# A gated feed-forward stage on one core: four raw weight buffers, a stated order, token sums on VectorE, and the bias table moved to the first block

## The chip, the core and the metric

The kernel runs on one core of a Trainium2 chip. Its engines work side by side, each through an instruction queue of its own and in order: TensorE (PE in the profile), VectorE (DVE), ScalarE (ACT), GpSimd (POOL), and SyncE (SP), which here only starts transfers. The metric is the device time of one execution, in microseconds. A median over runs is given for the kernel before; the profile shows one execution.

## The reference

One step of a decoder trunk with two layers over 576 tokens (512 of a prompt, 64 of samples) and 1024 features. The part that the change touches is the gated feed-forward block, which runs four times, and the relative bias of the attention.

```python
def rms_norm(x, g):
    xf = x.astype(jnp.float32)
    y = xf * lax.rsqrt(jnp.mean(xf * xf, axis=-1, keepdims=True) + RMS_EPS)
    return (y * g.astype(jnp.float32)).astype(x.dtype)

def swiglu(x, wi, wo):
    gate, up = jnp.split(x @ wi, 2, axis=-1)
    return (jax.nn.silu(gate) * up) @ wo
...
        bias = rel_bias[t5_buckets(offs)][:, g * ATTN_HEADS:(g + 1) * ATTN_HEADS].astype(f32)
...
        h = h + 0.5 * swiglu(rms_norm(h, w['norm_w'][i, 0]), w['ffn1_wi'][i], w['ffn1_wo'][i])
...
        h = h + mix
        h = h + 0.5 * swiglu(rms_norm(h, w['norm_w'][i, 2]), w['ffn2_wi'][i], w['ffn2_wo'][i])
        h = h + jax.nn.sigmoid(rms_norm(h, w['norm_w'][i, 3]) @ w['pe_gate'][i]) * (p[i] @ w['pe_proj'][i])
```

The inner width is 2816, that is 22 tiles of 128. Layer 0 mixes by a recurrence (RWKV), layer 1 by windowed attention with three groups of windows; `bias` is the table of relative biases of one group.

## The kernel before

**Tiling.** Activations lie with features on the 128 partitions and the 576 tokens along the row, in two halves of 288 (`HF`). Every float32 operand is split in two parts, H (a rounded copy, made by ScalarE's cast) and L (the rest, a subtraction), and a product is three matmuls: H with H, H with L, L with H. So each raw weight tile of 128 x 512 costs a transfer (SyncE), a cast (ScalarE) and a subtraction (GpSimd, or VectorE for some).

**Stages.** `run` (L1653) goes: block A (first feed-forward of layer 0), RWKV, block B (second of layer 0), the gated extra input and the shared keys and values, block C (first of layer 1), attention, block D (second of layer 1), final norm. All four blocks are `ffn` (L352).

**A block.** The 22 pairs of a gate tile and an up tile come in order. Pairs 0 to 4 are plain (`pair`, L359): gate and up products into the four banks `ps_e`, VectorE evicts the gate sums times rs (L364), ScalarE takes silu (L150), GpSimd multiplies by rs again (L367), VectorE multiplies into the up sums (L370). Pairs 0 and 4 go through all four banks at once, so they need all four free. During pairs 0 to 4, `forms` (L283) prepares token sums for what follows: two scalings (L294) and four subtractions for each of four feature pairs, VectorE and GpSimd in turn (L296 to L299), and their splits (L157).

Pairs 5 to 21 (`pair7`, L379) do the 2 x 2 block product in seven products (L389) instead of eight. `seven` (L314) loads four raw blocks (L324: two from the three buffers `wr`, which the plain weights share, two from the three buffers `sr`), makes sums of weights s1, s2 and s4 on VectorE (L336) and s3 on GpSimd (L345), and splits the seven forms (casts L330 on ScalarE, subtractions L331). A pair's evictions are, in order: copies L395, L398, L401 on ScalarE, L403 on VectorE, L406 and L408 on VectorE, silu L150, L411 on GpSimd and L412 on VectorE. The banks of these products are the same `ps_e`, and two of another pool `ps_d`.

After pairs 7, 14 and 21 an output part (`wo_part`, L415) multiplies the finished tiles by their output weights (L168, L171, L172, L198, and L421 adds to the residual). The pair loop runs one pair ahead of it: pair 7 is done before the first output part, pair 8 comes behind it.

**The bias table.** `bias_table` (L1278) is called three times in block B, after pairs 2, 5 and 8. Each call makes 1160 columns in four chunks of 290: a one-hot chunk is loaded from ScalarE's queue (L1285, one buffer), one matmul into `ps_q` (L1287), a copy to `tb` (L1288), then a transfer of the table (L1289), and two reversed halves by copy (L1293) and transfer (L1294).

**Order.** A scheduler with a priority heap lays out each engine's queue at build time, from the order in which the code is written and from when operands and buffers come free in its plan. What an engine does next on the chip is that fixed order: an instruction that waits holds all behind it on its engine. Besides, the code can state an order between two instructions by hand.

## Time and profile before

| | us |
|---|---|
| median of three runs | 2956.97 (2955.53 to 2964.45) |
| the profiled execution | 2955.22 |
| its span in the trace | 2953.4 |
| busy: PE, POOL, DVE, ACT | 2757.3, 1568.7, 1528.6, 1299.3 |
| block A, pairs to last output part | about 30 to 444 |
| block B | about 1130 to 1563 |
| block C | about 1647 to 2067 |
| block D | about 2471 to 2888 |

How to read it: the table's last four lines are places in the span. TensorE's busy time also counts the slow stretches, in which its granted clock (PEclk in a window's row) is 0.50. A row of waits tells who released the waiting instruction last; the engine named may itself have waited for another.

### The profile page before, as it was taken

What the parts mean: (1) busy time and instruction counts of PE and PEld (TensorE: products, weight loads), DVE (VectorE), ACT (ScalarE), POOL (GpSimd) and SP (SyncE); (2) the same over time, 40 slices, a digit from 0 to 9 for tenths busy, and PEclk for the clock granted to TensorE, in tenths of its full rate; (3) what the DMA queues carried; (4) which work ended last, traced back from release to release, by engine and by line L of the source; (5) the groups of instructions that cost most, each with busy time, mean ns of one, the idle gap of its engine ahead of it and who ended that gap; (6) DMA issues with size and microseconds to landing.
All of it is one profiled execution on the core that took longest, in us unless ns stands there. A gap on an engine that the chain in (4) does not pass through costs nothing.

```text
span 2953.4 us, 56222 instructions
## 1 busy us (share of the span) xinstructions
PE 2757.3 (93%) x21958; PEld 2565.7 (87%) x21958; DVE 1528.6 (52%) x3192; ACT 1299.3 (44%) x2532; POOL 1568.7 (53%) x1300
## 2 busy tenths in 40 slices
PE   7899997998999999999999989999899999899997
PEld 7899996986767778889999989999888889899997
DVE  6432428557677756433436543243477775533435
ACT  4443435444333324434445444354455655434444
POOL 6655647544243337656654566564544326756653
PEclk9999998998999999999999999999999999999999
DMA  3222234222112112222233222223433443232223
GB/s 117 75 89 84 87 95 145 65 68 54 53 45 77 42 49 77 76 82 85 91 94 101 88 76 93 80 86 108 125 81 98 127 151 109 70 90 86 93 79 101
DMA packets 177580, 257.83 MB, mean 87 GB/s; under 512 B 47037, under 2 KB 71537, under 8 KB 177313
## 3 DMA queue, kind: packets, MB, share of 16 engines
q1 hardware_dynamic: 148736, 223.56, 25.4%
q10 hardware_dynamic: 28576, 30.66, 3.8%
q8 instruction: 173, 2.83, 0.4%
q14 instruction: 95, 0.77, 0.1%
HBM read 234.31 MB, written 19.85 MB: 86 GB/s over the span
## 4 chain that ended last, share of the span: by engine, by line
PE 70%; DVE 11%; issue 6%; POOL 6%; DMA 4%; ACT 3%; SPq 0%; DVEq 0%; ACTq 0%; POOLq 0%
PE ps_e L198 25%; PE ps_e L389 20%; PE ps_d L516 9%; PE ps_d L389 3%; PE ps_i L516 2%; PE ps_q L516 2%; PE ps_s L516 2%; PE ps_w L516 2%; POOL wl L172 1%; POOL wl L331 1%; PE ps_x L516 1%; PE ps_o L516 1%; PE ps_d L198 1%; DVE S L1303 1%; PE ps_pt L525 1%
## 5 line engine op out<-in xcount | busy, mean ns | idle before, releaser
L172 POOL TENSOR_TENSOR wl<-wr,wh 128x512 fp32r<-128x512 f32 (+2 forms) x477 | 598.9, 1265 | 694.4 <-ACT wh L171 653.9
L198 PE MATMUL ps_e<-hv,wh 128*128 128x288 f32 x2944 | 588.5, 295 | 2.5 <-ACT wh L171 1.3
L171 ACT CAST wh<-wr 128x512 fp32r<-128x512 f32 (+2 forms) x477 | 277.1, 586 | 573.6 <-PE ps_e L198 298.0
L198 PEld LDWEIGHTS ps_e<-hv,wh 128*128 128x128 f32 x2944 | 472.9, 188 | 3.8 <-POOL hv L157 2.2
L198 PE MATMUL ps_e<-hv,wl 128*128 128x288 f32 x1472 | 434.2, 295 | 1.2 <-POOL wl L172 1.2
L198 PE MATMUL ps_e<-x,wh 128*128 128x288 f32 x1792 | 371.0, 302 | 25.3 <-DVE u L370 12.8
L516 PE MATMUL ps_d<-x,wh 128*128 128x288 f32 x1664 | 369.1, 309 | 7.5 <-DVE q L1371 3.8
L198 PEld LDWEIGHTS ps_e<-x,wh 128*128 128x128 f32 x1792 | 296.3, 193 | 30.3 <-issue 15.2
L516 PEld LDWEIGHTS ps_d<-x,wh 128*128 128x128 f32 x1664 | 274.7, 192 | 28.1 <-issue 9.5
L198 PEld LDWEIGHTS ps_e<-hv,wl 128*128 128x128 f32 x1472 | 276.8, 188 | 1.5 <-POOL wl L172 1.4
L198 PE MATMUL ps_e<-x,wl 128*128 128x288 f32 x896 | 268.4, 300 | 1.6 <-POOL wl L172 1.6
L389 PE MATMUL ps_e<-x,wh 128*128 128x288 f32 x1088 | 230.2, 305 | 31.5 <-DVE ev L406 18.4
L421 DVE SCALAR_TENSOR_TENSOR h<-ps_e,h 128x288 f32<-128x288 f32 x192 | 87.6, 456 | 325.9 <-PE ps_e L198 325.7
L516 PE MATMUL ps_d<-x,wl 128*128 128x288 f32 x832 | 250.6, 302 | 0.3 <-POOL wl L172 0.3
L389 PEld LDWEIGHTS ps_e<-x,wh 128*128 128x128 f32 x1088 | 180.8, 195 | 37.0 <-DVE ev L406 21.4
L331 POOL TENSOR_TENSOR wl<-wr,wh 128x512 fp32r<-128x512 f32 x136 | 177.8, 1310 | 11.1 <-ACT wh L330 9.9
L330 ACT CAST sh<-ps_q 128x512 fp32r<-128x512 f32 x136 | 79.9, 588 | 222.3 <-DVE ps_q L336 184.7
L331 POOL TENSOR_TENSOR wl<-ss,wh 128x512 fp32r<-128x512 f32 x68 | 88.6, 1302 | 166.4 <-ACT wh L330 156.4
L198 PEld LDWEIGHTS ps_e<-x,wl 128*128 128x128 f32 x896 | 172.4, 193 | 2.1 <-POOL wl L172 2.0
L389 PE MATMUL ps_e<-TH,wh 128*128 128x288 f32 x544 | 162.2, 298 | 12.9 <-ACT ev L395 11.2
L389 PE MATMUL ps_e<-x,wl 128*128 128x288 f32 x544 | 164.8, 303 | 0.0
L331 DVE TENSOR_TENSOR wl<-ps_q,wh 128x512 fp32r<-128x512 f32 x68 | 47.0, 691 | 222.2 <-ACT wh L330 222.2
(394 smaller groups left out, 6700.8 us busy)
## 6 DMA issues: line engine op xcount, KB each, us to landing
wr<-in_f1wi SPq DMA_DIRECT2D x108, 256.0 KB
wr<-in_f2wi SPq DMA_DIRECT2D x108, 256.0 KB
sr<-in_f1wi SPq DMA_DIRECT2D x68, 256.0 KB
sr<-in_f2wi SPq DMA_DIRECT2D x68, 256.0 KB
wr<-in_f1wo SPq DMA_DIRECT2D x64, 256.0 KB
wr<-in_f2wo SPq DMA_DIRECT2D x64, 256.0 KB
wr<-in_wrkv SPq DMA_DIRECT2D x48, 256.0 KB
wr<-in_wq SPq DMA_DIRECT2D x48, 256.0 KB
```

Of the source, the lines that this page charges most:

```text
L171: nc.scalar.copy(H, raw)
L172: nc.gpsimd.tensor_tensor(L, raw, H.bitcast(F32), op=ALU.subtract)
L198: nc.tensor.matmul(ps[0:nw], a, b[:, sl], start=k + m == 0, stop=3 * k + m == n - 1)
L330: nc.scalar.copy(H, a)
L331: eng.tensor_tensor(L, a, H.bitcast(F32), op=ALU.subtract)
L389: nc.tensor.matmul(ps, a, b, start=first and k + m == 0, stop=k == DT // 2 - 1 and m == 2, skip_group_check=True)
L421: nc.vector.scalar_tensor_tensor(h[:, sl], ps, 0.5, h[:, sl], op0=ALU.mult, op1=ALU.add)
L516: self.nc.tensor.matmul(out, lhsT, rhs, **kw)
L525: self.nc.tensor.transpose(out, in_, ident)
L1303: nc.vector.tensor_tensor_reduce(dst, ps, bias, -1.0, 3.0e38 if mx is None else mx, op0=ALU.add, op1=ALU.min, accum_out=m)
```

## The change

It does four things. The raw buffers `wr` and `sr` go from three to four. A stated order (`after`) puts each pair's s1 behind the last up eviction of the pair two before on VectorE, its first cast behind that pair's silu on ScalarE, its s3 behind that pair's last split on GpSimd, and half of the first splits of the quarters behind pair 4's last up eviction. The token sums are VectorE's alone (their splits GpSimd's), and so is the product t*rs of the plain pairs. The bias table is made in block A, after pairs 9, 12 and 16, in three chunks of 387 into `ps_d`, with the one-hot rows of a group loaded by one transfer ahead, and one reversed copy.

```diff
+B_MID = (9, 12, 16)
...
+    def after(self, ins, other):
+        self.tc.add_manual_dep(ins, other.name, mybir.DependencyInfo(mybir.DependencyClass.NoSync, mybir.DependencyReason.DATA), reason="order")
...
-            raw = self.wp.tile([128, c * nw], F32, name="wr", tag="wr", bufs=N_W - 1)
+            raw = self.wp.tile([128, c * nw], F32, name="wr", tag="wr", bufs=N_W)
...
             nc.vector.tensor_tensor(c[:, h0], a[:, h1], a[:, h0], op=sub)
-            nc.gpsimd.tensor_tensor(c[:, h1], b[:, h1], a[:, h1], op=sub)
+            nc.vector.tensor_tensor(c[:, h1], b[:, h1], a[:, h1], op=sub)
             nc.vector.tensor_tensor(d, b[:, h1], c[:, h0], op=sub)
-            nc.gpsimd.tensor_tensor(a[:, h1], b[:, h0], d, op=sub)
+            nc.vector.tensor_tensor(a[:, h1], b[:, h0], d, op=sub)
...
-            self.split(d, H[:, 2], L[:, 2])
+            self.split(d, H[:, 2], L[:, 2], nc.gpsimd)
...
-                    self.split(xn[k][z], H, L, (nc.vector, nc.gpsimd)[k % 2])
+                    if k % 2:
+                        self.split(xn[k][z], H, L, nc.gpsimd)
+                    else:
+                        nc.scalar.copy(H, xn[k][z])
+                        i = nc.vector.tensor_tensor(L, xn[k][z], H.bitcast(F32), op=sub).ins
+                        if z:
+                            self.after(i, self.last_u)
...
-    def seven(self, w0, w1):
+    def seven(self, w0, w1, prev):
...
-                r = self.ph.tile([128, n], F32, name="sr", tag="sr", bufs=3)
+                r = self.ph.tile([128, n], F32, name="sr", tag="sr", bufs=N_W)
             else:
-                r = self.wp.tile([128, n], F32, name="wr", tag="wr", bufs=N_W - 1)
+                r = self.wp.tile([128, n], F32, name="wr", tag="wr", bufs=N_W)
...
-            nc.scalar.copy(H, a)
+            c = nc.scalar.copy(H, a).ins
+            if not i and prev:
+                self.after(c, prev[1])
...
+            if op == ALU.add and prev:
+                self.after(i, prev[0])
...
+        if prev and prev[2]:
+            self.after(i, prev[2])
...
                 if half:
-                    self.act(t1, t1, AF.Silu)
-                    nc.gpsimd.tensor_tensor(t1, t1, rs, op=ALU.mult)
+                    hist[j] = [self.act(t1, t1, AF.Silu)]
+                    (nc.vector if fast else nc.gpsimd).tensor_tensor(t1, t1, rs, op=ALU.mult)
...
+            hist[j] = self.last_u, hist[j][0], None
...
-            W = self.seven(wi[j], wi[FT + j])
+            W = self.seven(wi[j], wi[FT + j], hist[j - 2])
...
+            hist[j] = i, silu, self.last_l
...
-                if mid and j in (2, 5, 8):
-                    mid(j // 3)
+                if mid and j in B_MID:
+                    mid(B_MID.index(j))
...
+    def bias_rows(self, g):
+        self.oh = self.sm("oh", [33, TBW])
+        self.nc.scalar.dma_start(self.oh, self.I["onehot"][g])
...
-        for c in range(0, TBW, 290):
-            e = min(c + 290, TBW)
-            oh = self.sm("oh", [33, 290])
-            nc.scalar.dma_start(oh[:, 0:e - c], self.I["onehot"][g][:, c:e])
-            ps = self.bank("q", e - c)
-            nc.tensor.matmul(ps[0:16], self.rb[:, g * 16:(g + 1) * 16], oh[:, 0:e - c], start=True, stop=True)
+        for c in range(0, TBW, 387):
+            e = min(c + 387, TBW)
+            ps = self.pg.tile([128, e - c], F32, name="ps_d", tag="d")
+            nc.tensor.matmul(ps[0:16], self.rb[:, g * 16:(g + 1) * 16], oh[:, c:e], start=True, stop=True)
             nc.vector.tensor_copy(tb[:, c:e], ps[0:16])
+        if g < 2:
+            self.bias_rows(g + 1)
         nc.scalar.dma_start(self.tab[g * 16:(g + 1) * 16], tb)
-        n = SKW // 2
-        for c in (0, n):
-            tr = self.sm("tr", [16, n])
-            nc.vector.tensor_copy(tr, tb[:, TBW - 1 - c - n:TBW - 1 - c][:, ::-1])
-            nc.scalar.dma_start(self.rev[g * 16:(g + 1) * 16, c:c + n], tr)
+        tr = self.sm("tr", [16, SKW])
+        nc.vector.tensor_copy(tr, tb[:, TBW - 1 - SKW:TBW - 1][:, ::-1])
+        nc.scalar.dma_start(self.rev[g * 16:(g + 1) * 16], tr)
...
-            self.ffn(I["f1wi"][0], I["f1wo"][0], lambda: self.feed(spill=True), pre, fast="n00")
+            self.bias_load()
+            self.ffn(I["f1wi"][0], I["f1wo"][0], lambda: self.feed(spill=True), pre, self.bias_table, fast="n00")
...
-                self.bias_load()
-                self.ffn(I["f2wi"][0], I["f2wo"][0], lambda: self.feed("n03"), self.pre, self.bias_table, fast="n02")
+                self.ffn(I["f2wi"][0], I["f2wo"][0], lambda: self.feed("n03"), self.pre, fast="n02")
```

Line numbers move: the changed kernel has L300 to L305 for the sums (L294 to L299 before), L336 for the raw loads (L324), L345 for the splits (L331), L350 for s1, s2 and s4 (L336), L361 for s3 (L345), L382 for the gate eviction (L364), L385 for t*rs (L367), L388 for the up eviction (L370), L408 for the seven products (L389), L414, L417, L420, L422, L425, L427 and L431 for the evictions of a seven-product pair (L395, L398, L401, L403, L406, L408, L412), and L441 for the output parts (L421).

**VectorE around pair 3 in block A.** The numbers behind a name tell one tile from another: hv_607 and hv_608 (hv_614 and hv_615 in the changed kernel) are the scaled features of the last token sums, t1_623 (t1_630) the gate tile of pair 3, u_624 (u_631) its up tile. Before:

```order
L294 SCALAR_TENSOR_TENSOR hv_607<-h1_104,vecs_66,rs_165 128x576
L298 TENSOR_TENSOR u_596<-hv_592,t1_595 128x288
L294 SCALAR_TENSOR_TENSOR hv_608<-h3_146,vecs_66,rs_165 128x576
L296 TENSOR_TENSOR t1_611<-hv_607 128x288
L157 TENSOR_TENSOR TL2_602<-u_596,TH2_601 128x288
L298 TENSOR_TENSOR u_612<-hv_608,t1_611 128x288
L364 TENSOR_TENSOR t1_623<-ps_e_649,rs_165 128x288
L364 TENSOR_TENSOR t1_623<-ps_e_675,rs_165 128x288
L157 TENSOR_TENSOR TL3_618<-u_612,TH3_617 128x288
L370 TENSOR_TENSOR u_624<-ps_e_703,t1_623 128x288
```

The same place now:

```order
L300 SCALAR_TENSOR_TENSOR hv_614<-h1_104,vecs_66,rs_165 128x576
L305 TENSOR_TENSOR hv_598<-hv_599,u_603 128x288
L300 SCALAR_TENSOR_TENSOR hv_615<-h3_146,vecs_66,rs_165 128x576
L302 TENSOR_TENSOR t1_618<-hv_614 128x288
L303 TENSOR_TENSOR t1_618<-hv_615,hv_614 128x288
L304 TENSOR_TENSOR u_619<-hv_615,t1_618 128x288
L382 TENSOR_TENSOR t1_630<-ps_e_656,rs_165 128x288
L305 TENSOR_TENSOR hv_614<-hv_615,u_619 128x288
L382 TENSOR_TENSOR t1_630<-ps_e_682,rs_165 128x288
L385 TENSOR_TENSOR t1_630<-t1_630,rs_165 128x576
L388 TENSOR_TENSOR u_631<-ps_e_710,t1_630 128x288
```

The two splits (TL) have left VectorE; the subtractions L303 and L305 and the product L385 have come, one L305 between the two gate evictions.

**SyncE's queue behind the first output part of block A.** The names wr and sr are raw weights; 1833, 1835, 1837 and 1839 are pair 8's four blocks, 1983 to 1989 pair 9's, and from 2133 pair 10's (in the changed kernel 1840 to 1846, 1990 to 1996, and from 2156). Before:

```order
L168 DMA wr_1775<-in_f1wo 128x512
L168 DMA wr_1781<-in_f1wo 128x384
L324 DMA wr_1833<-in_f1wi 128x512
L324 DMA wr_1837<-in_f1wi 128x512
L324 DMA wr_1983<-in_f1wi 128x512
L324 DMA sr_1989<-in_f1wi 128x512
L324 DMA wr_1987<-in_f1wi 128x512
L324 DMA sr_2135<-in_f1wi 128x512
L324 DMA sr_2139<-in_f1wi 128x512
```

The same place now:

```order
L174 DMA wr_1782<-in_f1wo 128x512
L174 DMA wr_1788<-in_f1wo 128x384
L336 DMA wr_1840<-in_f1wi 128x512
L336 DMA wr_1844<-in_f1wi 128x512
L336 DMA sr_2158<-in_f1wi 128x512
L336 DMA wr_1990<-in_f1wi 128x512
L336 DMA wr_1994<-in_f1wi 128x512
L336 DMA wr_2156<-in_f1wi 128x512
L336 DMA sr_2162<-in_f1wi 128x512
```

Both `sr` blocks of pair 9 are loaded before the output weights now, a block of pair 10 stands ahead of pair 9's two `wr` blocks, and these two follow each other.

**VectorE in pair 8.** 2145 (2168 in the changed kernel) is s1 of pair 10; 1949, 1877 and 1878 (1956, 1884 and 1885) are what pair 8's evictions write. Before:

```order
L403 TENSOR_TENSOR t1_1877<-ps_d_1881,ev_1894 128x288
L336 TENSOR_TENSOR ps_q_2145<-sr_2135,wr_2137 128x512
L331 TENSOR_TENSOR sl_2020<-ps_q_2017,sh_2019 128x512
L406 TENSOR_TENSOR ev_1949<-ps_e_1879,ev_1908 128x288
L408 TENSOR_TENSOR t1_1877<-ps_e_1880,ev_1922 128x288
L331 TENSOR_TENSOR sl_2148<-ps_q_2145,sh_2147 128x512
L336 TENSOR_TENSOR ps_q_2151<-ps_q_2145,wr_2133 128x512
L412 TENSOR_TENSOR u_1878<-ps_e_1879,t1_1877 128x288
```

The same place now:

```order
L422 TENSOR_TENSOR t1_1884<-ps_d_1888,ev_1901 128x288
L345 TENSOR_TENSOR sl_2027<-ps_q_2024,sh_2026 128x512
L425 TENSOR_TENSOR ev_1956<-ps_e_1886,ev_1915 128x288
L427 TENSOR_TENSOR t1_1884<-ps_e_1887,ev_1929 128x288
L431 TENSOR_TENSOR u_1885<-ps_e_1886,t1_1884 128x288
L350 TENSOR_TENSOR ps_q_2168<-sr_2158,wr_2160 128x512
L345 TENSOR_TENSOR sl_2171<-ps_q_2168,sh_2170 128x512
```

The first sums of pair 10's weights stood among pair 8's evictions and stand behind the last of them now.

## Rows read from the trace of the kernel before

**Rows 1.** The page's first part: busy time, share of the span, instructions of each engine.

```profile
PE 2757.3 (93%) x21958; PEld 2565.7 (87%) x21958; DVE 1528.6 (52%) x3192; ACT 1299.3 (44%) x2532; POOL 1568.7 (53%) x1300
```

**Rows 2.** Waits of PE, whole run: waiting line, its releaser, total us, times, longest.

```profile
PE ps_e L389 <- DVE ev L406: 18.4, 11, 3.3
...
PE ps_e L389 <- DVE t L364: 13.1, 3, 4.9
PE ps_e L198 <- DVE u L370: 12.8, 4, 4.2
PE ps_e L389 <- ACT ev L395: 11.2, 8, 2.1
...
PE ps_q L1287 <- DMA oh<-in_onehot: 7.7, 5, 1.9
...
PE ps_e L198 <- ACT TH L156: 2.8, 3, 1.1
...
PE ps_q L1287 <- DVE tb L1288: 2.1, 1, 2.1
```

**Rows 3.** Windows: us; busy of PE, PEld, DVE, ACT, POOL; PEclk, DMA share, GB/s.

```profile
76.03:82.86 6.83, 5.40 (x22) 5.43 (x23) 2.70 (x3) 1.34 (x2) 5.06 (x4) 0.50 0.17 46
...
192.09:195.50 3.41, 3.41 (x16) 3.41 (x15) 1.53 (x3) 1.50 (x3) 1.20 (x2) 0.50 0.25 77
...
sum 68.26, PE 57.45 PEld 53.12 DVE 37.08 ACT 26.48 POOL 37.02; mean PE 4.42 PEld 4.09 DVE 2.85 ACT 2.04 POOL 2.85
```

**Rows 4.** Timeline, end of pair 3: start, us, engine, line, operation, [idle before <-releaser].

```profile
61.36 1.53 DVE L157 TENSOR_TENSOR hv<-u,hv 128x576 fp32r<-128x576 f32 x1 [0.74 <-ACT hv L156]
...
69.18 1.55 DVE L157 TENSOR_TENSOR TL<-u,TH 128x288 fp32r<-128x288 f32 x1
...
71.63 0.81 DVE L364 TENSOR_TENSOR t<-ps_e,rs 128x288 f32<-128x288 f32 x2
...
72.85 0.68 ACT L150 ACTIVATE t<-t 128x576 f32<-128x576 f32 x1
...
75.43 1.39 POOL L367 TENSOR_TENSOR t<-t,rs 128x576 f32<-128x576 f32 x1
...
76.86 0.82 DVE L370 TENSOR_TENSOR u<-ps_e,t 128x288 f32<-128x288 f32 x2 [2.51 <-POOL t L367]
...
77.46 0.82 PE L198 MATMUL ps_e<-x,wh 128*128 128x288 f32 x2 [4.21 <-DVE u L370]
```

**Rows 5.** Timeline of DVE, pair 4.

```profile
93.50 0.90 DVE L336 TENSOR_TENSOR ps_q<-sr,wr 128x512 f32<-128x512 f32 x1 [1.69 <-DMA wr<-in_f1wi]
...
95.66 0.81 DVE L364 TENSOR_TENSOR t<-ps_e,rs 128x288 f32<-128x288 f32 x2
```

**Rows 6.** Timelines of four engines, first pairs after an output part.

```profile
172.07 0.70 DVE L336 TENSOR_TENSOR ps_q<-sr,wr 128x512 f32<-128x512 f32 x1 [5.01 <-DMA wr<-in_f1wi]
...
175.24 1.30 POOL L331 TENSOR_TENSOR wl<-wr,wh 128x512 fp32r<-128x512 f32 x1
...
176.57 0.33 SPq L324 DMA_DIRECT2D wr<-in_f1wi  x1
...
179.72 0.70 DVE L336 TENSOR_TENSOR ps_q<-sr,wr 128x512 f32<-128x512 f32 x1 [2.98 <-DMA wr<-in_f1wi]
...
182.95 0.40 PE L389 MATMUL ps_e<-TH,wh 128*128 128x288 f32 x1 [2.08 <-ACT ev L395]
...
189.94 0.70 DVE L336 TENSOR_TENSOR ps_q<-sr,wr 128x512 f32<-128x512 f32 x1 [2.89 <-DMA wr<-in_f1wi]
```

**Rows 7.** Single lines: count, ns min/median/max, first and last start, forms.

```profile
L298 DVE TENSOR_TENSOR u<-hv,t x16: 446/696/1146, 40.2 to 2517.0; 128x288 f32<-128x288 f32 x16
...
L367 POOL TENSOR_TENSOR t<-t,rs x20: 1387/1430/1515, 33.5 to 2546.5; 128x576 f32<-128x576 f32 x20
```

**Rows 8.** Timeline of ACT's queue, one group of the bias table.

```profile
1214.34 6.22 ACTq L1285 DMA_DIRECT2D oh<-in_onehot  x3
```

**Rows 9.** Timeline of DVE, pair 7, no stall.

```profile
131.70 0.46 DVE L408 TENSOR_TENSOR t<-ps_e,ev 128x288 f32<-128x288 f32 x1 [1.16 <-PE ps_e L389]
```

More of the change, by code (lines that the diff above doesn't have):

```diff
@@ L152, in act @@
         self.agrp.append(i)
+        return i
+    def after(self, ins, other):
+        self.tc.add_manual_dep(ins, other.name, mybir.DependencyInfo(mybir.DependencyClass.NoSync, mybir.DependencyReason.DATA), reason="order")
     def split(self, src, H, L, eng=None):
@@ L156, in split @@
         nc.scalar.copy(H, src)
-        (eng or nc.vector).tensor_tensor(L, src, H.bitcast(F32), op=ALU.subtract)
+        self.last_l = (eng or nc.vector).tensor_tensor(L, src, H.bitcast(F32), op=ALU.subtract).ins
         return H, L
@@ L335, in diff @@
             t = self.bank("q")
-            nc.vector.tensor_tensor(t, a, b, op=op)
+            i = nc.vector.tensor_tensor(t, a, b, op=op).ins
+            if op == ALU.add and prev:
+                self.after(i, prev[0])
             return t
@@ L344, in seven @@
         s3 = self.ph.tile([128, n], F32, name="ss", tag="ss", bufs=1)
-        nc.gpsimd.tensor_tensor(s3, raw["11"], raw["21"], op=ALU.subtract)
+        i = nc.gpsimd.tensor_tensor(s3, raw["11"], raw["21"], op=ALU.subtract).ins
+        if prev and prev[2]:
+            self.after(i, prev[2])
         form(4, s3, nc.gpsimd)
@@ L355, in ffn @@
         xs, rs = self.xl[0], self.rs
-        hv = {}
+        hv, hist = {}, {}
         self.n_hv, self.n_t1 = N_HF, 4
@@ L365, in ev_g @@
                 if half:
-                    self.act(t1, t1, AF.Silu)
-                    nc.gpsimd.tensor_tensor(t1, t1, rs, op=ALU.mult)
+                    hist[j] = [self.act(t1, t1, AF.Silu)]
+                    (nc.vector if fast else nc.gpsimd).tensor_tensor(t1, t1, rs, op=ALU.mult)
             def ev_u(half, ps, sl):
-                nc.vector.tensor_tensor(u[:, sl], ps, t1[:, sl], op=ALU.mult)
+                self.last_u = nc.vector.tensor_tensor(u[:, sl], ps, t1[:, sl], op=ALU.mult).ins
             last = fast and j == F_STD - 1
@@ L408, in pair7 @@
             nc.vector.tensor_tensor(t1[:, h1], C, u2, op=ALU.add)
-            self.act(t1, t1, AF.Silu)
+            silu = self.act(t1, t1, AF.Silu)
             prod(A, 6, 3, False)
             nc.gpsimd.tensor_tensor(u[:, h1], c22, t1[:, h1], op=ALU.mult)
-            nc.vector.tensor_tensor(u[:, h0], A, t1[:, h0], op=ALU.mult)
+            i = nc.vector.tensor_tensor(u[:, h0], A, t1[:, h0], op=ALU.mult).ins
             hv[j] = self.split(u, self.s("hv", self.n_hv, F32R), self.s("hv", self.n_hv, F32R), nc.gpsimd)
+            hist[j] = i, silu, self.last_l
         def wo_part(js, last):
@@ L720, in weights @@
                 if n not in wl:
-                    raw = self.wp.tile([128, 512], F32, name="wr", tag="wr", bufs=N_W - 1)
+                    raw = self.wp.tile([128, 512], F32, name="wr", tag="wr", bufs=N_W)
                     H = self.wp.tile([128, 512], F32R, name="wh", tag="wh")
@@ L1276, in bias_load @@
         self.rev = self.dr.tile([48, SKW], F32, name="rev")
+        self.bias_rows(0)
+    def bias_rows(self, g):
+        self.oh = self.sm("oh", [33, TBW])
+        self.nc.scalar.dma_start(self.oh, self.I["onehot"][g])
     def bias_table(self, g):
         nc = self.nc
+        oh = self.oh
         tb = self.sm("tb", [16, TBW])
-        for c in range(0, TBW, 290):
-            e = min(c + 290, TBW)
-            oh = self.sm("oh", [33, 290])
-            nc.scalar.dma_start(oh[:, 0:e - c], self.I["onehot"][g][:, c:e])
-            ps = self.bank("q", e - c)
-            nc.tensor.matmul(ps[0:16], self.rb[:, g * 16:(g + 1) * 16], oh[:, 0:e - c], start=True, stop=True)
+        for c in range(0, TBW, 387):
+            e = min(c + 387, TBW)
+            ps = self.pg.tile([128, e - c], F32, name="ps_d", tag="d")
+            nc.tensor.matmul(ps[0:16], self.rb[:, g * 16:(g + 1) * 16], oh[:, c:e], start=True, stop=True)
             nc.vector.tensor_copy(tb[:, c:e], ps[0:16])
+        if g < 2:
+            self.bias_rows(g + 1)
         nc.scalar.dma_start(self.tab[g * 16:(g + 1) * 16], tb)
-        n = SKW // 2
-        for c in (0, n):
-            tr = self.sm("tr", [16, n])
-            nc.vector.tensor_copy(tr, tb[:, TBW - 1 - c - n:TBW - 1 - c][:, ::-1])
-            nc.scalar.dma_start(self.rev[g * 16:(g + 1) * 16, c:c + n], tr)
+        tr = self.sm("tr", [16, SKW])
+        nc.vector.tensor_copy(tr, tb[:, TBW - 1 - SKW:TBW - 1][:, ::-1])
+        nc.scalar.dma_start(self.rev[g * 16:(g + 1) * 16], tr)
     def softmax(self, S, parts, n, adds):
```

## The prediction

> **What bounds the kernel now.** I read the page's busy line first: TensorE is busy 93% of the span and every other engine about half of it [rows 1]. So the time is TensorE's work plus TensorE's holes, and the change takes away none of that work. Next come TensorE's waits over the whole run [rows 2]. Five of the lines belong to the gated feed-forward blocks (four of them, called A to D in order): the last sums of a product that VectorE has not evicted (L406, 18.4 us), gate sums not evicted (L364, 13.1), up sums not evicted (L370, 12.8), copies by ScalarE not done (L395, 11.2), and in block B alone a one-hot chunk not landed (L1287, 7.7) or a table copy late (2.1). With L156 (2.8) that is 68.4 us, all of it in stretches which the change touches. Third is the granted clock. In 13 stretches of the four blocks it is 0.50, the 1.2 GHz level, and they begin in or right after such holes [rows 3]: two of the holes below end at 77.46 and near 192, and stretches begin at 76.03 and 192.09. TensorE was busy for 57.45 us in them; at 2.4 GHz that work takes half, so the holes cost 28.7 us a second time.
>
> Then the timeline around three holes, for who is late and why.
>
> **Start of the seven-product pairs** (blocks A, C, D, and hidden in B). TensorE has finished pair 3, and pair 4 wants four banks at once. VectorE evicts the gate sums only at 71.63, since the token sums fill it; silu runs at 72.85; the product t*rs stands on GpSimd behind two splits and runs at 75.43; the up sums leave at 76.86 and TensorE goes on at 77.46 [rows 4]. A pair later VectorE stands in front of s1 of pair 6, which waits for its raw weights until 93.50, and the gate eviction behind it comes at 95.66 [rows 5].
>
> **First pairs after an output part** (twice in each block). The raw buffer that s1 of pair 9 needs is free when GpSimd has split pair 8's (175.24 + 1.30 = 176.54), its load is issued at 176.57, and s1 runs at 179.72. ScalarE's cast of s1 is queued ahead of its copy L395 of pair 8, so TensorE waits 2.08 us. At 189.94 s1 of pair 10 is late in the same way, and VectorE's L406 stands behind it [rows 6].
>
> **The change, part by part.**
>
> *Token sums and t*rs.* Between the up sums of pair 2 and the last gate eviction of pair 3, VectorE has four scalings, four subtractions and one split; now four scalings and seven subtractions, with the splits on GpSimd. A subtraction on VectorE is 0.70 us (median of L298 [rows 7]) and the split was 1.55: 3 x 0.70 - 1.55 = +0.6 us [rows 4]. So the gate sums leave no earlier than before, rather 0.6 us later, silu at about 73.4. What is won is behind it: t*rs runs directly on VectorE. Its price there is not in the trace; its nearest rows are L157's split of the same size on VectorE at 61.36 (1.53 us, from beside a busy GpSimd [rows 4]) and twice the shortest half-size subtraction, 2 x 0.45 = 0.9 [rows 7]; I take 1.5, the row of the same size. The up sums then leave at 73.4 + 0.7 + 1.5 = 75.6 instead of 76.86, and the hole of 1.1 + 4.2 = 5.3 becomes about 4.0. GpSimd is now free of 32 subtractions and 20 products of 1.43 us [rows 7], and with less beside it I let VectorE's four scalings run 0.2 us faster each (an estimate; L298 alone spreads by 0.7): I take 3.2. Bounds: 5.3, if nothing runs faster and t*rs takes 2 us or more; 1.4, if VectorE is not late at all and the up sums wait only for themselves, silu and t*rs at 0.9. The other products t*rs (four of five per block) lie beside the matmuls of a whole pair, and cost nothing while VectorE is half idle [rows 1]; without that cover each is 1.5 us.
>
> *Stated order, pairs 5 and 6.* s1 of pair 6 now follows the up sums of pair 4, so the gate eviction no longer stands behind a load. The hole of 4.4 us (13.1 over three [rows 2]) falls to about 0.7, one eviction and one cast. Per block 3.2 + 0.7 = 3.9; A, C, D go from 13.1 + 12.8 + 2.8 = 28.7 to 11.7: **-17.0**. Block B has hardly any of this now, because its bias work fills the place (there TensorE waits for other things); with the bias gone it takes the shape of the others, 3.9, less 1.5 for small waits that the bias work causes behind it (an estimate): **+2.4**.
>
> *Four raw buffers and the stated order, after output parts.* With a fourth buffer, the load for s1 of pair 9 waits for the split of an output weight, which GpSimd does before pair 8's; it is queued on SyncE behind a load that waits for s1 of pair 8, which runs at 172.07 even today [rows 6]. From issue to s1 I take today's 179.72 - 176.57 = 3.15 us, behind 172.1. I put s1 of pair 9 at about 175.3 where it was 179.72; the copy L395 is then ready just before TensorE asks for it. s1 of pair 10 stands behind the last eviction of pair 8, so L406 can't wait for its load. L406 and L395 hold 18.4 + 11.2 = 29.6 us in 19 waits; I leave 0.2 each, 3.8: **-25.8**. Bounds: nothing left, or all of it.
>
> *Bias table.* Three groups move from B to A. TensorE's own work stays (twelve matmuls of 290 columns against nine of 387: the same columns). In B its waits of 7.7 + 2.1 us go. In A the one-hot rows of a group are loaded ahead by one transfer, so the load of each chunk, of which TensorE waited up to 1.9 us, falls away. What takes its place: ScalarE's queue now issues next rows, table and reversed rows in one run, and stands until the copies on VectorE are done; ScalarE's copies for TensorE are behind that. Today a run of three issues takes 6.22 us [rows 8], with loads between them; without them I put the delay at 0 to 2.5 us a group and take 0.9: 2.7 in all. **-7.1**. The rb and first one-hot loads at the start of A go to a stretch in which TensorE waits for weights anyway; 0 to 1 us, taken at 0.
>
> *Clock.* With holes of 3 us in four places and under 1 us elsewhere, I leave one stretch at 0.50 as the shortest in the trace (3.41 us, half lost, 1.7) per block and one for the bias: 5 x 1.7 = 8.5 of 28.7. **-20.2**. Bounds: 0 left, and one in each old place, 13 x 1.7 = 22.
>
> Sum: -17.0 + 2.4 - 25.8 - 7.1 - 20.2 = **-67.7 us**. The profiled execution took 2955.2 us (span 2953.4), so 2887.5; the median of the runs is 1.8 higher, and I say **2888**.
>
> **The rivals.**
>
> *VectorE gains nothing from taking over the sums.* Rows of one kind differ by more than two to one: L298 takes from 0.45 to 1.15 us, median 0.70 [rows 7]. If all seven subtractions run at 1.05 and t*rs at 2 us, the up sums leave at 76.9 as before and all four blocks keep the 5.3 us hole with a longer slow-clock stretch: 4 x (2.1 + 0.5) = 10 more, 2898. The Trainium skill, "SBUF — State Buffer", section "Who interferes with whom", says that a VectorE instruction with two SBUF inputs and a GpSimd instruction that reads SBUF lock each other out for a whole instruction. By that rule the moved subtractions and t*rs are of the kind that is blocked while GpSimd splits weights, and the time would be this rival's 2898 rather than 2888; the spread of L298 agrees with it, but not how often. Chance 0.17.
>
> *The loads stay late.* SyncE works its queue in order, and the new order puts a load of pair 10 (its buffer is free only after s1 of pair 8) ahead of both loads of pair 9. If that holds them as the missing buffer does now, the 25.8 us come back, with four slow stretches: 2888 + 25.8 + 4 x 1.7 = 2921. For it: the wait at 179.72 is one for a load. Against: s1 of pair 8 is done before 173 even today [rows 6]. Chance 0.12.
>
> *Slower: the stated order makes every pair late.* s1 of pair j may not start before the last eviction of pair j-2. In the 68 seven-product pairs evictions follow each other by a product, 1.62 us (1.16 idle and 0.46 for L408 [rows 9]). If s1 (0.70 [rows 6]) and its cast, taken like ScalarE's silu (0.68 [rows 4]), then stand in front of a copy that is due, each pair costs up to 1.38 us: 68 x 1.38 = 94, 2982. It turns slower at 1.0 us a pair. Against: a copy has a product, 1.62 us, until its bank is asked for, and with s1, the cast and no more in front of it some 0.2 us remains in hand. Chance 0.08.
>
> *The bias delays A.* 2.5 us and a slow stretch for each of three groups: 3 x (1.6 + 1.7) - 1.7 = 8 more, 2896. Chance 0.08, worked out as if alone.
>
> **How the numbers follow.** Forecast 0.55, the others 0.17 (no gain on VectorE), 0.12 (late loads), 0.08 (bias) and 0.08 (slower order). The forecast's own bounds: low, the hole at 1.4 (4 x -1.8 = -7), no bias delay (-2.7), nothing after output parts (-3.8), no slow stretch (-8.5): -22 in all, 2866; high, the first and last of the faster rivals together, 2906. The late loads at 2921 must be inside for 8 in 10 to hold, so the range is 2866 to 2926. Within 0.3% (9 us, what a measurement of this kernel can tell from no change) needs the slower order to cost 0.9 to 1.1 us a pair: 0.03 of its 0.08; slower 0.05; faster 0.92. Outside the range lie the slower order, a third of the late loads and a small low tail, under 0.2 together.
>
> **What would show it.** In the changed trace: waits for L425 and L414 (the old L406 and L395) under 5 us in all; no wait for one-hot rows; the up sums of pair 3 near 75.6 us, and the hole before pair 4 near 3 us; s1 of pair 9 near 175; five or fewer slow stretches in the four blocks; TensorE's busy time down by about 20 us, by clock alone. It is wrong if waits show inside pairs 10 to 14, where there are none today, or if s1 of pair 9 still starts at 179.

## The result

The changed kernel takes 2881.5 us (median of four, 2875.3 to 2887.4) against 2959.8 of the kernel before on the same chip (median of four): a ratio of 0.9735, 95% interval 0.9705 to 0.9764, or 78 us less. The forecast was 2888, 69 less than the median it started from. The profiled execution of the changed kernel took 2887.4 us, its span is 2885.6, so it is the slowest of the four, where the one of before (2955.2) lies below all of its runs: the two traces differ by 67.8 us and not by 78. All that follows by traces accounts for the 67.8.

The page of the changed kernel, busy time and share of the span, answers to [rows 1]:

```profile
PE 2743.1 (95%) x21952; PEld 2560.1 (89%) x21952; DVE 1563.4 (54%) x3222; ACT 1299.6 (45%) x2532; POOL 1553.0 (54%) x1264
```

TensorE's busy time has fallen by 14.2 us with the same columns to multiply; 13.0 of it is the clock in the four blocks, as the windows below show. The other 54 us were idle time between its matmuls. Its waits over the whole run (total, times, longest), where the seven lines of [rows 2] add up to 68.1 us (the prediction's 68.4 is a slip in the sum):

```profile
PE ps_e L408 <- ACT ev L420: 13.7, 4, 3.4
...
PE ps_e L204 <- DVE u L388: 8.6, 4, 2.2
...
PE ps_e L204 <- DVE t L382: 3.5, 4, 0.9
```

These three lines, 25.8 us, stand where the seven stood. L406 and L395 (now L425 and L414) and the one-hot rows do not appear. The first line is new: in [rows 2] it had no counterpart of that size.

The timeline of the hole before pair 4, VectorE with one GpSimd row and TensorE's (start, us, line), answers to [rows 4]:

```profile
56.29 0.46 DVE L388 TENSOR_TENSOR u<-ps_e,t 128x288 f32<-128x288 f32 x1 [2.74 <-PE ps_e L204]
...
58.73 1.54 DVE L300 SCALAR_TENSOR_TENSOR hv<-h,vecs,rs 128x576 f32<-128x576 f32 x2
...
60.56 0.45 DVE L303 TENSOR_TENSOR t<-hv 128x288 f32<-128x288 f32 x1
...
65.01 2.97 POOL L178 TENSOR_TENSOR wl<-wr,wh 128x512 fp32r<-128x512 f32 x2
...
65.29 1.54 DVE L303 TENSOR_TENSOR t<-hv 128x288 f32<-128x288 f32 x1
66.75 1.54 DVE L304 TENSOR_TENSOR u<-hv,t 128x288 f32<-128x288 f32 x1
...
69.82 0.45 DVE L382 TENSOR_TENSOR t<-ps_e,rs 128x288 f32<-128x288 f32 x1
71.02 1.38 DVE L385 TENSOR_TENSOR t<-t,rs 128x576 f32<-128x576 f32 x1 [0.75 <-ACT t L151]
72.53 0.82 DVE L388 TENSOR_TENSOR u<-ps_e,t 128x288 f32<-128x288 f32 x2
...
73.14 0.58 PE L204 MATMUL ps_e<-x,wh 128*128 128x288 f32 x1 [2.15 <-DVE u L388]
```

The rows of before for the first two (up sums of pair 2, first scaling of the last token sums):

```profile
59.80 0.82 DVE L370 TENSOR_TENSOR u<-ps_e,t 128x288 f32<-128x288 f32 x2 [4.23 <-POOL t L367]
...
62.81 1.54 DVE L294 SCALAR_TENSOR_TENSOR hv<-h,vecs,rs 128x576 f32<-128x576 f32 x2
```

Block A starts 2.2 us earlier in this trace, so 69.82 is where the gate sums left before (71.63 plus a row's 0.4). As forecast, nothing was won ahead of them, but by two changes that cancel. Measured from the start of the block, the scalings begin 1.9 us earlier (58.73 for 62.81), since pair 2's up sums wait no more for t*rs on GpSimd; and from there to the last gate eviction VectorE is busy 11.5 us instead of 9.6. What was won is t*rs right behind silu, 1.38 us instead of a place in GpSimd's queue. One instruction, L303, takes 0.45 us where GpSimd stands and 1.54 where it works.

The new hole, in pair 5 (VectorE, ScalarE, TensorE):

```profile
90.56 2.81 DVE L320 TENSOR_TENSOR x<-hv,x 128x576 fp32r<-128x576 f32 x2
93.30 1.84 DVE L163 TENSOR_TENSOR hv<-u,hv 128x576 fp32r<-128x576 f32 x1
95.06 1.75 DVE L350 TENSOR_TENSOR ps_q<-sr,wr 128x512 f32<-128x512 f32 x1
...
96.85 0.59 ACT L342 CAST sh<-ps_q 128x512 fp32r<-128x512 f32 x1 [5.19 <-DVE ps_q L350]
97.33 0.40 ACT L420 COPY ev<-ps_e 128x288 f32<-128x288 f32 x1
...
97.78 0.40 PE L408 MATMUL ps_e<-TH,wh 128*128 128x288 f32 x1 [3.42 <-ACT ev L420]
```

s1 of pair 6 (95.06) waits for no load any more. It stands on VectorE behind two splits of the quarters (L320) and pair 4's own split (L163), ScalarE's cast of it comes after 5.19 us of idling, and the copy L420 of pair 5 that TensorE needs is queued behind the cast.

The first pair after an output part, answers to [rows 6]:

```profile
168.30 0.70 DVE L350 TENSOR_TENSOR ps_q<-sr,wr 128x512 f32<-128x512 f32 x1 [0.76 <-DMA wr<-in_f1wi]
...
171.08 0.42 PE L408 MATMUL ps_e<-x,wh 128*128 128x288 f32 x2
...
173.29 0.39 ACT L414 COPY ev<-ps_e 128x288 f32<-128x288 f32 x1
```

s1 of pair 9 runs 2.8 us before pair 8's first product (171.08), where before it ran inside the pair, and the copy L414 is not behind anything that waits.

The slow stretches inside the four blocks, first two and sum of eight (us; busy of PE, PEld, DVE, ACT, POOL; clock), answer to [rows 3]:

```profile
72.05:78.88 6.83, 5.75 (x24) 5.78 (x25) 6.53 (x8) 3.13 (x5) 4.74 (x4) 0.50 0.35 116
99.36:102.77 3.41, 3.41 (x17) 3.41 (x16) 1.72 (x4) 1.28 (x3) 1.54 (x2) 0.50 0.40 111
...
sum 34.14, PE 31.44 PEld 31.53 DVE 27.82 ACT 16.82 POOL 21.27; mean PE 3.93 PEld 3.94 DVE 3.48 ACT 2.10 POOL 2.66
```

Two in each block, one in or behind each hole; 57.45 us of slow work have become 31.44, worth 13.0 us.

### The profile page after: what moved, and what is told of

Read it like the earlier page. It is cut to its first block, busy times and chain, and to the rows that moved or that the text cites. A ratio compares the mean times of both kernels' runs of the same rounds, so it can differ in the third digit from the quotient of the medians.

```text
span 2885.6 us, 56048 instructions
## 1 busy us (share of the span) xinstructions
PE 2743.1 (95%) x21952; PEld 2560.1 (89%) x21952; DVE 1563.4 (54%) x3222; ACT 1299.6 (45%) x2532; POOL 1553.0 (54%) x1264
## 3 DMA queue, kind: packets, MB, share of 16 engines
q1 hardware_dynamic: 148736, 223.56, 25.8%
## 4 chain that ended last, share of the span: by engine, by line
PE 51%; DVE 5%; ACT 2%; issue 1%; DMA 1%; POOL 0%; DVEq 0%; ACTq 0%; POOLq 0%
PE ps_e L204 23%; PE ps_e L408 16%; PE ps_d L536 5%; PE ps_d L408 3%; PE ps_s L536 2%; PE ps_o L536 1%; PE ps_pt L545 1%; DVE S L1332 1%; DVE S L1327 1%; DVE hv L300 0%; ACT wh L177 0%; ACT QS L1401 0%; DVE hv L163 0%; DVE t L385 0%; ACT t L151 0%
## 5 line engine op out<-in xcount | busy, mean ns | idle before, releaser
L178 POOL TENSOR_TENSOR wl<-wr,wh 128x512 fp32r<-128x512 f32 (+2 forms) x477 | 607.5, 1283 | 721.6 <-ACT wh L177 681.7
L204 PE MATMUL ps_e<-x,wh 128*128 128x288 f32 x1792 | 373.0, 304 | 23.0 <-DVE u L388 8.6
L441 DVE SCALAR_TENSOR_TENSOR h<-ps_e,h 128x288 f32<-128x288 f32 x192 | 87.6, 457 | 335.6 <-PE ps_e L204 335.4
L408 PE MATMUL ps_e<-x,wh 128*128 128x288 f32 x1088 | 219.8, 295 | 0.0
L345 POOL TENSOR_TENSOR wl<-wr,wh 128x512 fp32r<-128x512 f32 x136 | 196.0, 1444 | 23.1 <-ACT wh L342 16.8
L408 PEld LDWEIGHTS ps_e<-x,wh 128*128 128x128 f32 x1088 | 174.6, 188 | 3.9 <-issue 3.9
L408 PE MATMUL ps_e<-TH,wh 128*128 128x288 f32 x544 | 162.0, 298 | 13.7 <-ACT ev L420 13.7
L536 PEld LDWEIGHTS ps_d<-x,wl 128*128 128x128 f32 x832 | 160.5, 193 | 2.0 <-issue 0.5
L408 PE MATMUL ps_e<-TH,wl 128*128 128x288 f32 x544 | 161.3, 296 | 0.0
L408 PE MATMUL ps_e<-TL,wh 128*128 128x288 f32 x544 | 160.7, 295 | 0.0
L408 PE MATMUL ps_e<-x,wl 128*128 128x288 f32 x544 | 159.8, 295 | 0.0
```

The source lines that it names most:

```text
L178: nc.gpsimd.tensor_tensor(L, raw, H.bitcast(F32), op=ALU.subtract)
L204: nc.tensor.matmul(ps[0:nw], a, b[:, sl], start=k + m == 0, stop=3 * k + m == n - 1)
L345: eng.tensor_tensor(L, a, H.bitcast(F32), op=ALU.subtract)
L408: nc.tensor.matmul(ps, a, b, start=first and k + m == 0, stop=k == DT // 2 - 1 and m == 2, skip_group_check=True)
L441: nc.vector.scalar_tensor_tensor(h[:, sl], ps, 0.5, h[:, sl], op0=ALU.mult, op1=ALU.add)
L536: self.nc.tensor.matmul(out, lhsT, rhs, **kw)
```

## The experiments

To compare kernels stage by stage I use the length of a block in its trace, from the start of its first gate eviction (L364; L382 changed) to the end of its last output eviction (L421; L441). Block A before: 31.91 to 443.78, 411.9 us; changed: 29.72 to 432.46, 402.7. The four blocks sum to 1647.8 us before and 1581.4 changed, 66.4 of the 67.8. A version has one trace, and what two traces of one kernel differ by in the blocks was not measured. Outside the blocks the traces below lie between 1289 and 1308 us, so a difference of a few us counts only where rows show its cause. Ratios are to runs of the kernel before on the same chip; the changed kernel's is 0.9735.

The theory at the outset: each late row has its own cause, the late load cured by the fourth buffer, the eviction behind a load by the stated order, the late t*rs by the move to VectorE. The rivals: one of the parts does it all, or does nothing.

### Three buffers again

```diff
-                r = self.ph.tile([128, n], F32, name="sr", tag="sr", bufs=N_W)
+                r = self.ph.tile([128, n], F32, name="sr", tag="sr", bufs=3)
...
-                r = self.wp.tile([128, n], F32, name="wr", tag="wr", bufs=N_W)
+                r = self.wp.tile([128, n], F32, name="wr", tag="wr", bufs=N_W - 1)
```

The two other places that make a `wr` tile have the same edit.

> The changed kernel with three raw buffers wr and sr again; the stated order stays. If the fourth buffer is what brings the load for s1 of pair 9 forward (my theory), TensorE waits for the copy L414 again in the first pair after an output part, in eight places at 1 to 2 us, 11 us in all, and not for L425, since s1 of pair 10 stays behind pair 8's evictions; with two or three more slow stretches about 2895 us. Rival, the stated order alone removes these waits: none after output parts, 2881 us.

Ratio 0.9819 (0.9792 to 0.9845); blocks 1591.6. Its waits of TensorE:

```profile
PE ps_e L408 <- ACT ev L420: 13.7, 4, 3.4
...
PE ps_e L408 <- ACT ev L414: 8.4, 8, 1.6
```

The L414 wait is back in exactly the eight places after output parts (0.8 to 1.6 us), and L425 is not: the fourth buffer is what removes the first of the two waits in the changed kernel, and the order can remove the second without it. Its price was put at 11 us, it is 8.4, and 10.2 in the blocks.

### No stated order

```diff
     def after(self, ins, other):
...
-        self.tc.add_manual_dep(ins, other.name, mybir.DependencyInfo(mybir.DependencyClass.NoSync, mybir.DependencyReason.DATA), reason="order")
+        return
```

> The changed kernel without the stated order (after() does nothing); four buffers stay. If the order is what keeps a wait for loads away from the evictions (my theory), the wait for the gate sums of pair 4 (4.4 us in three or four blocks) and some of the waits for L425 after output parts come back, while the wait of 3.4 us in pair 5 for L420 goes: about 2895 us. Rival, with four buffers the loads are early enough in any order: no L425 wait, about 2880 us.

Ratio 0.9745 (0.9718 to 0.9772); blocks 1575.8, so 5.6 us less than with the order. Whole runs show no difference: the intervals of the two ratios overlap.

```profile
PE ps_e L204 <- DVE u L388: 13.6, 8, 2.5
...
PE ps_e L408 <- ACT ev L420: 2.0, 4, 0.5
PE ps_e L408 <- DVE ev L425: 1.4, 4, 0.4
```

My expectation was wrong and the rival right. Neither the gate sums of pair 4 nor the evictions after output parts wait, and the 3.4 us hole in pair 5 is down to 0.5, with 0.4 for L425 behind it. At these two places the loads are there before s1 in any order once there are four buffers, and the order removes nothing. It does remove something else: without it s1 of pair 5 stands among the up evictions of pair 3, and the waits before pair 4 are 4.2 to 4.4 us in a block (0.9, 2.5 and 0.8 to 1.0) instead of 3.0. So the order wins 1.2 us or more there and loses 2.6 in pair 5.

### The token sums shared again

```diff
-            nc.vector.tensor_tensor(c[:, h1], b[:, h1], a[:, h1], op=sub)
+            nc.gpsimd.tensor_tensor(c[:, h1], b[:, h1], a[:, h1], op=sub)
...
-            nc.vector.tensor_tensor(a[:, h1], b[:, h0], d, op=sub)
+            nc.gpsimd.tensor_tensor(a[:, h1], b[:, h0], d, op=sub)
...
-            self.split(d, H[:, 2], L[:, 2], nc.gpsimd)
+            self.split(d, H[:, 2], L[:, 2])
```

> The changed kernel with the token sums shared between VectorE and GpSimd as before (and the split of the third sum on VectorE); t*rs stays on VectorE. If the two engines block each other while both read, it matters little who does the sums: the gate sums of pair 3 leave within 1 us of 69.8, the hole of 3.0 us before pair 4 stays between 2 and 4.5, 2878 to 2888 us. Rival, taking the sums to VectorE is what shortened this hole: it grows back to 5.3, 4 x 2.3 and slow stretches, about 2893 us.

Ratio 0.9761 (0.9731 to 0.9790), which overlaps the changed kernel's; blocks 1577.6. One wait before pair 4 instead of two, of the same length in sum:

```profile
PE ps_e L204 <- DVE u L388: 12.0, 4, 3.0
```

So taking the sums to VectorE alone won nothing that shows. The gate sums even leave 1.9 us earlier in the block than in the changed kernel (I expected less than 1); but t*rs then stands on VectorE behind a split and takes 1.81 us, and the up sums leave only 0.4 earlier.

### t*rs on GpSimd again

```diff
-                    (nc.vector if fast else nc.gpsimd).tensor_tensor(t1, t1, rs, op=ALU.mult)
+                    nc.gpsimd.tensor_tensor(t1, t1, rs, op=ALU.mult)
```

> The changed kernel with the product t*rs of the plain pairs on GpSimd again. My theory, the product behind two splits in GpSimd's queue made the hole before pair 4: it grows from 3.0 to about 5 us in four blocks, 2881 + 8 and a slow stretch or two, about 2891 us. Rival, GpSimd has been freed of so much else that it does the product in time: the hole stays near 3 us, 2881 us.

Ratio 0.9795 (0.9762 to 0.9827); blocks 1589.5. The hole before pair 4 is 5.5 us in block A (1.86, 0.86 and 2.79) and 4.5 to 4.9 in the others:

```profile
PE ps_e L204 <- DVE u L388: 10.7, 4, 2.8
...
PE ps_d L408 <- DVE x L320: 7.0, 8, 1.1
PE ps_e L204 <- ACT TH L162: 5.5, 4, 1.9
PE ps_e L408 <- DVE ev L425: 4.8, 4, 2.0
```

As expected before pair 4: of the part on token sums, this product is what shortened the hole. Not expected is pair 5. The wait for L420 is gone, since ScalarE has that copy ahead of the cast here; TensorE waits for the quarters' splits (L320) instead, 1.75 us in a block, which VectorE reaches late because pair 4's up sums waited for the product too (4.24 us in block A), and for L425 (0.4 to 2.0).

### Only the bias table moved

The bias part of the diff on the kernel before, nothing else.

> The kernel before with the bias table alone moved to the first block. By the prediction's term: block B loses its bias work and waits and takes the shape of the others, block A grows by the nine matmuls and 0 to 2.5 us a group: B from 422 to 406, A from 412 to 421 or 424, sum 1642, ratio 0.998. Rival, A's queues are blocked by the bias transfers on ScalarE's queue: A grows by more than 16 us, and the sum is that of before or more.

Ratio 0.9974 (0.9960 to 0.9988); blocks 1639.1, 8.7 less. B goes from 421.9 to 408.9, A from 411.9 to 418.4. A grows by 6.5 us. The nine matmuls are 18 rows of 0.49 us in the changed kernel's trace (median), 8.8 in all; against them stand 0.5 us less of holes and one slow stretch less (1.7), so little else is paid there. Two small waits for L406 (0.7 and 0.3), each behind an s1 that waits for its load, are new in A. The waits for one-hot rows are gone and B has the two 4 us waits of the other blocks. The term (-7.1 with +2.4 beside it, so -4.7 without the clock) was of this size: the holes of over 0.25 us fell by 4.6, and most of the rest is the clock.

### Bias table and buffers, bias table and order

The four buffers were not measured with the table left in block B, so what they do is known only on top of the move. Both kernels have token sums and t*rs as before; the first has four buffers and no order, the second three buffers and the order.

> The kernel before with only two parts of the change: the bias table in the first block and four raw buffers; no stated order, token sums and t*rs as before. After the run without the order I now think that the buffers alone clear every wait for a late load: none of the 2 to 3 us waits for L414 or L425 after output parts, none of 4 us for the gate sums of pair 4; the hole before pair 4 stays at 5 us since t*rs is on GpSimd. Blocks 1590 us in sum (before 1648, changed 1581), ratio 0.978 to before. My theory at the prediction, that the stated order carries half of it: gate-sum waits of 4 us and some L425 waits stay, blocks 1610 us, ratio 0.988.

Ratio 0.9800 (0.9776 to 0.9824); blocks 1593.7.

```profile
PE ps_e L204 <- DVE u L388: 29.1, 8, 4.2
PE ps_e L408 <- ACT ev L420: 4.5, 4, 1.2
```

VectorE in block A, between the two up evictions of pair 3:

```profile
75.20 0.46 DVE L388 TENSOR_TENSOR u<-ps_e,t 128x288 f32<-128x288 f32 x1 [2.51 <-POOL t L385]
76.47 1.70 DVE L350 TENSOR_TENSOR ps_q<-sr,wr 128x512 f32<-128x512 f32 x1 [0.82 <-DMA wr<-in_f1wi]
...
79.43 0.45 DVE L388 TENSOR_TENSOR u<-ps_e,t 128x288 f32<-128x288 f32 x1
```

> The kernel before with only the bias table in the first block and the stated order; three buffers, token sums and t*rs as before. If late loads are what makes the waits, the order only moves them from VectorE's evictions to ScalarE's copies: L414 after output parts 1 to 2 us in eight places, none for L425, 3.4 us in pair 5 for L420 in the place of the gate sums of pair 4, 5 us before pair 4: blocks 1605 us, ratio 0.986. Rival, the order alone clears the waits: blocks 1590 us, ratio 0.978.

Ratio 0.9837 (0.9810 to 0.9864); blocks 1601.5.

```profile
PE ps_e L204 <- DVE u L388: 16.8, 4, 4.2
PE ps_d L408 <- DVE x L320: 10.6, 7, 2.8
...
PE ps_e L408 <- ACT ev L414: 6.5, 9, 1.2
```

With the buffers alone, no wait after output parts and none for the gate sums of pair 4; both had been waits for a load. The 29.1 us are 4.2 and 3.1 in each block, before pair 4: the 4.2 are t*rs late from GpSimd, the 3.1 are s1 of pair 5 (76.47, after 0.82 of waiting for its load) and a split of it, which stand between the two up evictions of pair 3. I had expected 5 us there and it is 8. With the order alone, L425 after output parts and the gate sums are cleared too, and L414 is left. The 3.4 us for L420 that I expected in pair 5 are not there; as with t*rs on GpSimd above, TensorE waits for the quarters' splits (L320), 2.5 to 2.8 us in each block, so the order pays for the gate sums with another wait in the next pair. The two parts remove much the same waits by two ways: from the 1639.1 of the move alone, the buffers take 45 us and the order 38, and together with the sums and t*rs they take only 58.

### The two holes that are left

```diff
-            W = self.seven(wi[j], wi[FT + j], hist[j - 2])
+            p = hist[j - 2]
+            if j == F_STD + 1:
+                p = self.c22, p[1], p[2]
+            W = self.seven(wi[j], wi[FT + j], p)
...
-            nc.vector.tensor_tensor(c22, A, e5, op=ALU.add)
+            self.c22 = nc.vector.tensor_tensor(c22, A, e5, op=ALU.add).ins
```

> The changed kernel with one edit: s1 of pair 6 is stated behind pair 5's L425 instead of pair 4's last up eviction; the token sums keep their places. The 3.4 us hole in pair 5 goes and the 3.0 us hole before pair 4 stays: blocks 1581 - 4 x 3 - 5 of clock = 1564, ratio 0.969 to 0.970. Rival, pair 5 only waits for L425 or for the quarters' splits instead: 1575 or more, 0.973.

Ratio 0.9713 (0.9690 to 0.9735); blocks 1562.5. The hole of 3.4 us is gone from all four blocks, the two waits before pair 4 (0.9 and 2.2) stand as they were, and each block has one slow stretch instead of two. That is 18.9 us in the blocks for 13.7 us of hole; in whole runs the intervals of the two ratios still overlap. L420 was late only for the cast in front of it.

With this edit and one more:

```diff
-STEPS = ((0,), (1,), (2, 3), (), (4,))
+STEPS = ((0,), (1, 2), (3,), (), (4,))
```

> The changed kernel with two edits: s1 of pair 6 is stated behind pair 5's c22 eviction (L425) instead of pair 4's last up eviction, and the third token sums are made one pair earlier. If the 3.4 us hole in pair 5 is ScalarE's copy L420 behind the cast of a late s1, and the 3.0 us hole before pair 4 is VectorE filled by two token sums at once, both fall under 1 us in four blocks, with most of the slow stretches: 4 x (3.0 + 2.3) and 10 of clock, blocks 1550 us in sum, ratio 0.963. Rival, the holes move on to the next eviction (L425 in pair 5, the up sums of pair 2 or 3): blocks 1575 to 1585, ratio 0.973.

Ratio 0.9666 (0.9639 to 0.9693), 2852.0 us beside 2952.8 of before: 101 us less, faster than both kernels; blocks 1554.6. Of the waits in the blocks these are the ones over 1.5 us in sum:

```profile
PE ps_e L411 <- ACT x L319: 4.6, 4, 1.2
...
PE ps_d L411 <- DVE x L320: 3.0, 5, 0.8
...
PE ps_e L411 <- ACT ev L417: 1.6, 4, 0.4
```

In none of the four blocks is the granted clock below 1.00 (no stretch at 0.50 lies in them).

The second edit without the first, and without any stated order:

> The changed kernel without the stated order and with the third token sums made one pair earlier. The hole before pair 4 (0.9 + 2.5 + 0.8 us without the order) falls to about 1 us in four blocks, with a slow stretch each: blocks 1560 us in sum, ratio 0.969. Rival, VectorE is then late in pair 2 instead, and TensorE waits there: 1576, ratio 0.9745 as without the order alone.

Ratio 0.9732 (0.9703 to 0.9761); blocks 1577.1, no better than without the order alone. VectorE is not late in pair 2. The trace shows what is (VectorE, end of pair 3):

```profile
68.15 0.46 DVE L388 TENSOR_TENSOR u<-ps_e,t 128x288 f32<-128x288 f32 x1
73.42 0.70 DVE L350 TENSOR_TENSOR ps_q<-sr,wr 128x512 f32<-128x512 f32 x1 [4.81 <-DMA wr<-in_f1wi]
...
75.97 0.45 DVE L388 TENSOR_TENSOR u<-ps_e,t 128x288 f32<-128x288 f32 x1
```

s1 of pair 5 stands between the two up evictions of pair 3 and waits for its load, 4.81 us. It stood there with the buffers alone too (a wait of 0.82), and without the order alone, with its load landed. That is what the stated order is good for: in the version with both edits s1 of pair 5 stands behind both evictions, and its wait for the load costs TensorE nothing there. Last, both edits with the token sums shared:

> The kernel with both edits of the better version, and the token sums shared with GpSimd as before. If who does the sums matters little, it gives the 1555 us of the version without this, within 4 us, ratio 0.966. If the sums on VectorE are needed, a hole of 1 to 3 us comes back before pair 4 or in pair 2 or 3: 1560 to 1570. If GpSimd has room, less: 1550.

Ratio 0.9684 (0.9659 to 0.9709); blocks 1554.4: the same.

### Does GpSimd's work lengthen VectorE's?

In pair 4's weights, the low parts are copies made by ScalarE, so GpSimd's four subtractions a block are missing.

```diff
...
+            if nosub:
+                nc.scalar.copy(L, raw)
+            else:
                 nc.gpsimd.tensor_tensor(L, raw, H.bitcast(F32), op=ALU.subtract)
...
+                g = [self.load_w(wi[x], list(range(c, c + DT // 2)), nosub=True) for c in (0, DT // 2) for x in (j, FT + j)]
```

> The changed kernel with GpSimd's four subtractions for the weights of pair 4 left out in each block (the low parts are plain copies by ScalarE, so the values are off). In the changed kernel the token sums L303 and L304 take 0.45 us at 60.6 and 60.9, where GpSimd stands, and 1.54 at 65.3 and 66.8, where it splits these weights. If the two engines shut each other out, both rows fall to about 0.45, the gate sums of pair 3 leave some 2 us earlier and the hole before pair 4 falls from 3.0 to about 1 us in each block. Rival, the rows are long for a reason of VectorE's own: they stay at 1.5 and the hole at 3.0.

One execution of 2871.2 us; blocks 1563.6. L306 and L307 are L303 and L304 of the changed kernel, L385 is its gate eviction L382; VectorE in the same place:

```profile
61.76 1.99 DVE L303 SCALAR_TENSOR_TENSOR hv<-h,vecs,rs 128x576 f32<-128x576 f32 x1
63.67 1.06 DVE L305 TENSOR_TENSOR t<-hv 128x288 f32<-128x288 f32 x1
64.65 0.45 DVE L306 TENSOR_TENSOR t<-hv 128x288 f32<-128x288 f32 x1
65.02 0.45 DVE L307 TENSOR_TENSOR u<-hv,t 128x288 f32<-128x288 f32 x1
...
66.12 0.45 DVE L385 TENSOR_TENSOR t<-ps_e,rs 128x288 f32<-128x288 f32 x1
```

And over the whole run (ns, min/median/max of 16), the changed kernel and then this one:

```profile
L303 DVE TENSOR_TENSOR t<-hv x16: 443/446/1546, 38.3 to 2458.3; 128x288 f32<-128x288 f32 x16
```

```profile
L306 DVE TENSOR_TENSOR t<-hv x16: 444/446/451, 37.7 to 2447.2; 128x288 f32<-128x288 f32 x16
```

The rows fall from 1.54 to 0.45, the gate sums leave 3 us earlier in the block, and the hole before pair 4 is gone in all four blocks. The scaling at 61.76 and the subtraction at 63.67, beside which GpSimd still splits token sums, stay long. The Trainium skill ("SBUF — State Buffer", section "Who interferes with whom") states that a VectorE instruction with two SBUF inputs contends with a GpSimd instruction that reads SBUF. This run agrees, with a factor of 3.4 on the 128 x 288 subtraction; whether one engine waits out a whole instruction of the other is not shown by it.

## Why the prediction was right, and where it was not

The sum held: -67.7 forecast for the profile, -67.8 measured, with 78 between the medians. That it held to a tenth is luck. The terms held less well: a hole that I missed and a clock loss that I put too low were offset by terms in which I had left something and nothing was left, and by 8 us that no term has. By the holes of over 0.25 us in the blocks:

| term | forecast | measured |
|---|---|---|
| A, C, D: before pair 4 and gate sums, with pair 5's small waits | -17.0 | -11.9 |
| B: the same place | +2.4 | +4.9 |
| after output parts | -25.8 | -28.3 |
| bias table | -7.1 | -11.5 |
| clock | -20.2 | -13.0 |
| sum | -67.7 | -59.8 |
| pieces of under 0.25 us and outside the blocks | 0 | -8.0 |

Three waits for L406 that the forecast counted under output parts (1.4 us) lay in pair 5 and are in the first row of the measured column; the measured 11.5 of the bias has 1.7 us of waits behind the table that the forecast left out.

*The hole before pair 4* was right in size, 3.0 us (0.87 + 2.15) for 3.2, and in kind: the gate sums leave no earlier, t*rs on VectorE (1.38, forecast 1.5) makes the difference, as the run with t*rs on GpSimd shows. The way to that size was partly wrong. The forecast had the seven subtractions cost 0.6 us and faster scalings give 0.8 back; measured, VectorE's work up to the last gate eviction grew by 1.9 us. What paid for it was t*rs of pair 2, which the forecast put at nothing: on VectorE it lets the whole sequence start 1.9 us earlier. The rival that VectorE gains nothing was wrong as a forecast of the time, but its mechanism is real: it is why 0.45 us became 1.54, and in the run with the weight splits left out the gate sums leave 3.0 us earlier and the hole is gone.

*The stated order in pairs 5 and 6* is the step that failed. "s1 of pair 6 now follows the up sums of pair 4, so the gate eviction no longer stands behind a load": true, but the buffers had done that already, and the order left s1 behind the splits of the quarters and of pair 4, with its cast in front of L420. I had that mechanism as the slower rival, over all 68 pairs at 1.38 us; it came in one pair of each block at 3.4. It could have been read ahead from the build's order of VectorE's queue, which has two splits and one more (L320, L163) in front of s1 of pair 6, as the trace shows. I priced s1 against the gate sums and did not follow the cast behind it.

*Output parts and bias* were right; 0 was left of each where I left 3.8 and 2.7. The late-load rival (2921) did not come: s1 of pair 9 still waits 0.76 us for its load, but it runs at 168.30 and not near 175, 2.8 us before pair 8's first product, since s1 of pair 8 runs early as well (160.08, 11 us before pair 8 starts).

*The clock* was mis-sized: eight slow stretches and not five, since the new hole in pair 5 brought its own, and two of the four before pair 4 are 6.83 us long, not 3.41. Most of it follows from the same missed hole: taking that hole away took four stretches, by the run with s1 behind c22. The blocks lost 15.7 us to the clock, not 8.5, and TensorE's busy time fell by 14.2 us, not by about 20.

*What stays open.* 6.6 us of the blocks' 66.4 lie in pieces of under 0.25 us, and 1.4 outside the blocks; neither was followed, nor was the spread between the two medians and the two traces (78 and 68). What two traces of one kernel differ by is not known.

## What to carry to other kernels

A wait for a load that stands in front of evictions can be cured from either side, by a buffer or by order, and the gains don't add: before crediting both, ask what the second still finds. A stated order that lifts one instruction out of a queue leaves its dependants where they were: follow the cast or copy behind it on the next engine, one row further than the row that was late. And moving work from GpSimd to VectorE shortens a chain only as far as GpSimd's remaining work is out of the way of it.
